# The last FFN's second product by seven block products in three passes

## The chip, the cores and the metric

The kernel runs on one core of one Trainium2 chip. Five engines of that core appear in the profile: TensorE for matrix products (PE, with its weight loads as PEld), VectorE (DVE), ScalarE (ACT), GpSimd (POOL) and SyncE (SP), whose queue issues nearly all the DMA transfers. The metric is the device time of one execution in microseconds (us).

## The reference

The program is a trunk of two layers on 512 tokens of width 1024: a gated short convolution, an FFN, a state-space mixer and a second FFN, each between two RMS norms and scaled, shifted and gated from a conditioning vector. All values are float32. The change touches the last FFN alone:

```python
def swiglu_ffn(h, w_in, w_out):
    gate, up = jnp.split(h @ w_in, 2, axis=-1)
    return (jax.nn.silu(gate) * up) @ w_out
...
        h = rmsnorm(x, norm_g[i, 2]) * (1.0 + scale) + shift
        y = swiglu_ffn(h, f_w_in[i], f_w_out[i])
        x = x + gate * rmsnorm(y, norm_g[i, 3])
```

The hidden width is 2816. The first product is 512 x 1024 by 1024 x 5632 (gate and up together); the second is 512 x 2816 by 2816 x 1024.

## The kernel before, in words

**Products.** Every float32 matrix is used as a pair of float32r parts: hi, a rounded copy that ACT makes (L202 for weights, L829 for activations), and lo, the value less hi, a DVE subtraction (L203, L830). One block product is then three matmuls: hi by hi, hi by lo and lo by hi. A matmul takes a 128 x 128 stationary block and a moving block of up to 512 columns and adds into one PSUM tile of 128 x 512.

**First product.** The 2816 hidden channels are 22 chunks of 128. `ffn` takes them in 11 pairs; a pair needs two gate chunks and two up chunks, and each chunk (`in_chunk`, L272, lines L259 to L261) is 8 x 3 matmuls of 512 tokens against the weight tile `whl`, channels on the partitions. `load_w` (L205) loads 256 columns of the weights as one 1 MB transfer into a `wst` tile (two buffers) and splits it into two `whl` tiles (four buffers). After a chunk, ACT takes the silu (L826), DVE multiplies gate by up (L827), and ACT and DVE split the product into the tiles `ff` (L829, L830), which all stay in SBUF. The first gate and up chunks of the stage are begun while the layer before still ends, and their matmuls have a line of their own (`li`).

**Second product.** `out_begin` (L346) goes over the two halves of 512 output columns. For each half and each of the 22 chunks, `mm_tiles` (L353, lines L359 to L361) multiplies four token tiles of 128 (stationary, from `ff`) with a weight block of 128 x 512 (moving, from `whlo`): 2 x 22 x 4 x 3 = 528 matmuls. `load_wo` (L226) loads `f_w_out` in pieces of up to four chunks into `wsto` tiles (the `wst` buffers) and splits them into `whlo` tiles (the `whl` buffers). The last two chunks of the first half and the last four of the second are done token tile by token tile (L502), and after each tile ACT squares and sums both halves (L400), DVE multiplies by gate and norm weight (L404), takes the reciprocal root (L414 on ACT, L417) and adds to the residual (L421), and SP stores the rows (L423).

**Order.** Within PE's part the order is as the code writes it; in the closing part of a stage it is written out by hand for PE, ACT and DVE. Elsewhere a scheduler orders each engine's queue and inserts the waits. An engine runs its queue in order, so an instruction that waits holds all that stand behind it; this goes for the transfers on SP's queue too.

## Time and profile before

| what | value |
|---|---|
| time, median of 3 runs | 1392.14 us (1391.38 to 1392.56) |
| span of the profiled execution | 1390.8 us |
| mean granted TensorE clock | 0.996 |
| PE busy | 1368.9 us of the span |
| DVE busy, ACT busy | 832.2 us, 552.4 us |
| DMA | 190.35 MB, mean 137 GB/s |
| matmuls of both FFNs' second products (L359 to L361, `y<-whlo,ff`) | 3 x 352 |

A row of a group of instructions gives line, engine, operation, written tile <- read tiles, shape and count; then the busy time in us, the mean duration of one in ns, and the idle time just before them with what ended it. Matmuls overlap: a matmul's duration in such a row is longer than the distance from one start to the next, so costs of PE are taken from starts. A row of the view by stretches of time gives the stretch, its length, the busy time and count of each engine, the granted clock (1.00 is full), the share of the 16 DMA engines and the GB/s. A row of the view of waits says who waited for whom: us in total, times, longest.

### The profile page before, as it was taken

The page shows a single profiled execution, that of the slowest core. Times are in us where ns is not written, and L with a number is a line of the kernel's source. Part 1 is how long each engine was busy: PE and PEld are TensorE (multiplying, and loading weights), DVE is VectorE, ACT ScalarE, POOL GpSimd, SP SyncE. Part 2 cuts the span into 40 slices and gives each one's busy share as a digit, 9 for nine tenths or more (in the row PEclk, how much of TensorE's full clock was granted, in tenths as well). Part 3 has the DMA queues.
Part 4 walks back from the last instruction along what each step waited for, and adds up shares of the span by engine and source line. Part 5 has one row for each costly group of instructions (what it writes and reads, how often), then busy time and mean ns, then how long its engine had stood idle before and what let it go on. Part 6 is the DMA issues. An engine that isn't in the chain of part 4 may idle for free.

```text
span 1390.8 us, 17396 instructions
## 1 busy us (share of the span) xinstructions
PE 1368.9 (98%) x7039; PEld 1148.8 (83%) x7039; DVE 832.2 (60%) x1332; ACT 552.4 (40%) x827; POOL 1.5 (0%) x11
## 2 busy tenths in 40 slices
PE   8999999999999999999799999999999999999998
PEld 7788889888888888898688888888898888888886
DVE  5777756488775222759878888876673333332224
ACT  5432247222222211745765466643573222322212
POOL 0000000000000000000000000000000000000000
PEclk9999999999999999999999999999999999999999
DMA  9956671368683223415244432423413223322221
GB/s 313 317 175 223 221 239 42 120 210 287 219 272 122 91 91 98 118 48 179 70 133 136 129 98 83 131 76 107 137 60 106 91 91 101 109 93 91 91 91 61
DMA packets 154037, 190.35 MB, mean 137 GB/s; under 512 B 5845, under 2 KB 110949, under 8 KB 152933
## 3 DMA queue, kind: packets, MB, share of 16 engines
q1 hardware_dynamic: 149952, 176.47, 39.2%
q10 hardware_dynamic: 4004, 12.77, 2.8%
q8 instruction: 55, 0.90, 0.3%
q14 instruction: 26, 0.20, 0.1%
HBM read 186.98 MB, written 2.24 MB: 136 GB/s over the span
## 4 chain that ended last, share of the span: by engine, by line
PE 66%; DVE 1%; issue 0%; DVEq 0%; ACT 0%; ACTq 0%
PE ip L259 11%; PE ip L261 11%; PE ip L260 11%; PE y L359 8%; PE y L360 8%; PE y L361 8%; PE li L259 2%; PE li L261 2%; PE li L260 2%; PE yd L1092 1%; PE yo L1086 1%; PE cb L1036 1%; PE xtr L460 1%; PE ssg L1114 0%; PE xtok L1019 0%; PE st L1051 0%
## 5 line engine op out<-in xcount | busy, mean ns | idle before, releaser
L259 PE MATMUL ip<-h,whl 128*128 128x512 f32 x1096 | 434.2, 396 | 2.7 <-DVE cv L777 2.7
L261 PE MATMUL ip<-h,whl 128*128 128x512 f32 x1096 | 429.4, 392 | 6.6 <-DVE whl L203 6.6
L260 PE MATMUL ip<-h,whl 128*128 128x512 f32 x1096 | 428.2, 391 | 0.0
L261 PEld LDWEIGHTS ip<-h,whl 128*128 128x128 f32 x1096 | 206.6, 188 | 50.7 <-DVE whl L203 7.0
L259 PEld LDWEIGHTS ip<-h,whl 128*128 128x128 f32 x1096 | 206.8, 189 | 47.7 <-issue 5.6
L260 PEld LDWEIGHTS ip<-h,whl 128*128 128x128 f32 x1096 | 206.7, 189 | 43.2 <-issue 1.2
L203 DVE TENSOR_TENSOR whl<-wst,whl 128x1024 fp32r<-128x1024 f32 (+1 forms) x163 | 177.2, 1103 | 101.4 <-ACT whl L202 101.2
L202 ACT CAST whl<-wst 128x1024 fp32r<-128x1024 f32 (+1 forms) x163 | 152.1, 951 | 201.0 <-PE ip L261 121.6
L203 DVE TENSOR_TENSOR whlo<-wsto,whlo 128x1024 fp32r<-128x1024 f32 x68 | 83.3, 1225 | 181.3 <-ACT whlo L202 181.3
L202 ACT CAST whlo<-wsto 128x1024 fp32r<-128x1024 f32 x68 | 71.5, 1051 | 200.6 <-PE y L361 162.2
L359 PE MATMUL y<-whlo,ff 128*128 128x512 f32 x352 | 137.0, 389 | 0.0
L361 PE MATMUL y<-whlo,ff 128*128 128x512 f32 x352 | 136.9, 389 | 0.0
L360 PE MATMUL y<-whlo,ff 128*128 128x512 f32 x352 | 136.9, 389 | 0.0
L126 DVE SCALAR_TENSOR_TENSOR ada_acc<-ada_st,csil,ada_acc 128x512 f32<-128x512 f32 x140 | 104.8, 750 | 22.9 <-DMA ada_st<-in_ada_w_dram 20.0
L259 PE MATMUL li<-h,whl 128*128 128x256 f32 x288 | 83.2, 289 | 0.0
L827 DVE TENSOR_TENSOR g<-ip,g 128x512 f32<-128x512 f32 x40 | 27.6, 691 | 92.5 <-PE ip L261 92.4
L261 PE MATMUL li<-h,whl 128*128 128x256 f32 x288 | 81.6, 283 | 0.0
L260 PE MATMUL li<-h,whl 128*128 128x256 f32 x288 | 81.5, 283 | 0.0
L826 ACT ACTIVATE g<-ip 128x512 f32<-128x512 f32 x36 | 21.6, 599 | 145.9 <-PE ip L261 145.9
L361 PEld LDWEIGHTS y<-whlo,ff 128*128 128x128 f32 x352 | 66.1, 188 | 13.8
L359 PEld LDWEIGHTS y<-whlo,ff 128*128 128x128 f32 x352 | 66.1, 188 | 13.7
L360 PEld LDWEIGHTS y<-whlo,ff 128*128 128x128 f32 x352 | 66.1, 188 | 13.6
(215 smaller groups left out, 1623.2 us busy)
## 6 DMA issues: line engine op xcount, KB each, us to landing
ada_st<-in_ada_w_dram SPq DMA_DIRECT2D x96, 512.0 KB, 5.8
wst<-in_f_w_in_dram SPq DMA_DIRECT2D x44, 1024.0 KB, 5.2
wsto<-in_f_w_out_dram SPq DMA_DIRECT2D x20, 1024.0 KB, 4.9
wst<-in_m_w_in_dram SPq DMA_DIRECT2D x14, 1024.0 KB, 5.4
wst<-in_m_w_in_dram SPq DMA_DIRECT2D x20, 512.0 KB, 5.0
wst<-in_a_w_in_dram SPq DMA_DIRECT2D x9, 1024.0 KB, 6.2
csb<-cs_d ACTq DMA_DIRECT2D x8, 1024.0 KB, 6.2
wsto<-in_m_w_out_dram SPq DMA_DIRECT2D x7, 1024.0 KB, 4.9
```

The costliest lines, as they stand in the source:

```text
L126: dve.scalar_tensor_tensor(acc, w, csil[:, k:k + 1], acc, MUL, ADD)
L202: act.copy(dst[:, 0, :nk, :], src)
L203: dve.tensor_tensor(dst[:, 1, :nk, :], src, dst[:, 0, :nk, :].bitcast(F32), SUB)
L259: pe.matmul(dst, w_at(w, 0, kk), a[:, 0, sl], start=start, stop=False)
L260: pe.matmul(dst, w_at(w, 0, kk), a[:, 1, sl], start=False, stop=False)
L261: pe.matmul(dst, w_at(w, 1, kk), a[:, 0, sl], start=False, stop=stop)
L359: pe.matmul(pst, a[:, 0, tk], wt[:, 0, kk, :], start=k == 0, stop=False)
L360: pe.matmul(pst, a[:, 0, tk], wt[:, 1, kk, :], start=False, stop=False)
L361: pe.matmul(pst, a[:, 1, tk], wt[:, 0, kk, :], start=False, stop=k == K - 1)
L460: pe.transpose(pt[:, j * 256 + t * P:j * 256 + (t + 1) * P], self.xn[2 * hi + t][p // 2][:, c:c + P], ident)
L826: act.activation(g, psg, AF.Silu)
L827: dve.tensor_mul(g, psu, g)
```

## The change

`ffn(3, ...)` is replaced by a function `last_ffn`. Its first product has the same matmuls. Its second product is seen as a product of 2 x 2 blocks: tokens 0 to 255 and 256 to 511, even and odd chunks of the hidden width, left and right half of the output columns. Strassen's algorithm in Winograd's form makes it from seven block products in place of eight, with sums of blocks of both factors ahead and sums of products behind. A block product over one pair of chunks is two token tiles of 128 by one weight block of 128 x 512, with three matmuls each.

- **Activations** (`ff_pair`, L1260): for each pair of chunks DVE multiplies gate by up straight into tiles `za` and `zb` (L1269 to L1271) and makes four sums of 128 x 256 (L1273 to L1276). They stay whole here; the split into hi and lo comes later, and the `ff` splits (L829, L830) are gone.
- **Weights**: for each pair of chunks SP loads the four blocks of `f_w_out` into a `tb` tile (L1284, L1285; two buffers), DVE makes four sums in place (L1291 to L1294), and SP stores the tile to device memory as `td` (L1297). This goes on beside the first product.
- **Second product**: 22 items of 18 matmuls (L1386 to L1388). Pass one, items 0 to 10, holds three of the seven products in the accumulators `pa`, `pb`, `pz`, pass two, items 11 to 21, three more; pass three adds the seventh product, 66 matmuls, onto `pb`, one token tile after the other. Per item SP loads `r8` (two blocks, 512 KB) and `r4` (one block, 256 KB) from `td` or `f_w_out`; ACT and DVE split the three left factors (`a6`, 128 x 768), `r8` into `w8` and `r4` into `w4` (L1321 on ACT, L1322 on DVE). Items are made four ahead (`AHEAD`). In pass one the left factors of pass three (`a22`, 128 x 256) are split as well, in pass two its weights (`t4`, three pairs of chunks per loading).
- **Between passes**: after pass one ACT copies `pa` (negated, `np1`) and `pz` (`c22`) and DVE takes `nr1` = `np1` - `pb`; after pass two DVE takes `nr2` from `pb` (L1429). The remaining sums (L1442, L1443, L1479) and the norm, gate, residual and stores stand beside and behind pass three.

PE runs 5975 instruction rows instead of 6041: 528 matmul rows of the second product become 22 x 18 + 66 = 462, and no other row of PE differs.

SP's queue in the first product (`wst` are its weight tiles, `tb` and `td` the new tiles; on each row, the written tile <- the read one). Before, weight loads stood one behind the other:

```order
L211 DMA wst<-in_f_w_in_dram 128x8x256 x4
L301 DMA gg<-gate_d 128x1024
L211 DMA wst<-in_f_w_in_dram 128x8x256 x15
L229 DMA wsto<-in_f_w_out_dram 128x4x512 x9
```

Now:

```order
L211 DMA wst<-in_f_w_in_dram 128x8x256 x4
L1284 DMA tb<-in_f_w_out_dram 128x2x512
L1285 DMA tb<-in_f_w_out_dram 128x2x512
L1284 DMA tb<-in_f_w_out_dram 128x2x512
L1285 DMA tb<-in_f_w_out_dram 128x2x512
L1297 DMA td_8572<-tb 128x2048
L1297 DMA td_8573<-tb 128x2048
L1284 DMA tb<-in_f_w_out_dram 128x2x512
L1285 DMA tb<-in_f_w_out_dram 128x2x512
L211 DMA wst<-in_f_w_in_dram 128x8x256
L1284 DMA tb<-in_f_w_out_dram 128x2x512
L1285 DMA tb<-in_f_w_out_dram 128x2x512
```

A load of `tb`, a store of `td` and a load of `wst` now alternate until the eleven tiles are stored; the last six loads of `wst` stand in one row again.

DVE's queue at the end of the first product. `za` and `zb` with `ip` or `g` behind the arrow are the last pair's products and sums; `w_10033` and `w_10032` are item 0's `w4` and `w8`, `w_10049` and `w_10048` those of item 1, `a_10047` item 1's `a6`. Before, from the last pair's product on:

```order
L827 TENSOR_TENSOR g<-ip,g 128x512
L203 TENSOR_TENSOR whlo<-wsto,whlo 128x1024
L830 TENSOR_TENSOR ff_9908<-g,ff_9908 128x512
L203 TENSOR_TENSOR whlo<-wsto,whlo 128x1024 x18
```

Now:

```order
L1322 TENSOR_TENSOR w_10033<-r_10028,w_10033 128x512
L1271 TENSOR_TENSOR zb<-ip,g 128x2x256
L1322 TENSOR_TENSOR w_10032<-r_10027,w_10032 128x1024
L1273 TENSOR_TENSOR za<-zb 128x256
L1322 TENSOR_TENSOR a_10040<-zb,a_10040 128x256
L1274 TENSOR_TENSOR za<-za 128x256
L1276 TENSOR_TENSOR zb<-za,zb 128x256
L1275 TENSOR_TENSOR zb<-za,zb 128x256
L1322 TENSOR_TENSOR a_10047<-za,a_10047 128x768
L1322 TENSOR_TENSOR w_10049<-r_10044,w_10049 128x512
L1322 TENSOR_TENSOR w_10048<-r_10043,w_10048 128x1024
```

The last pair's product with `ip` waits for the last matmul of the first product; the split of item 0's `w8` stands behind it, and the last pair's sums stand between it and item 1's splits.

DVE's queue at the end of pass two (`w_10748`, `w_10769`, `w_10793` are weights of pass three, loaded together as `t_10723`; `nr` are the two `nr2`):

```order
L1322 TENSOR_TENSOR w_10748<-t_10723,w_10748 128x512
L1322 TENSOR_TENSOR w_10769<-t_10723,w_10769 128x512
L1322 TENSOR_TENSOR w_10793<-t_10723,w_10793 128x512
L1429 TENSOR_TENSOR nr_10796<-np_10440,pb 128x512
L1429 TENSOR_TENSOR nr_10798<-np_10441,pb 128x512
L1322 TENSOR_TENSOR w_10802<-t_10790,w_10802 128x512
L1322 TENSOR_TENSOR w_10805<-t_10790,w_10805 128x512
```

Nothing of this stood there before. PE's first matmul of pass three writes `pb` and waits for `nr2`, which stands behind three splits that wait for the loading of `t_10723`.

The diff, cut:

```diff
--- before.py
+++ after.py
@@ -1246,10 +1246,243 @@
...
+    def last_ffn(begun, pool):
+        w1, w2 = f_w_in[1], f_w_out[1]
+        h, lead_ps, rest, more = begun
+        lo, hi = HALVES
+        NG2 = NF // 2
+        za, zb = [], []
+        td = [dram.tile([P, 4, T], F32, name=f"td{g}") for g in range(NG2)]
+        built = []
+        def ff_pair(pss):
+            a = pool.tile([P, 3, 256], F32, tag="za", name="za", bufs=NG2)
+            b = pool.tile([P, 4, 256], F32, tag="zb", name="zb", bufs=NG2)
+            gs = []
+            for i in range(2):
+                g = t2("g")
+                act.activation(g, pss[i], AF.Silu)
+                gs.append(g)
+            dve.tensor_mul(a[:, 0, :], pss[2][:, lo], gs[0][:, lo])
+            dve.tensor_mul(b[:, 1, :], pss[2][:, hi], gs[0][:, hi])
+            dve.tensor_mul(b[:, 0:4:3, :], pss[3].rearrange("p (a f) -> p a f", a=2),
+                           gs[1].rearrange("p (a f) -> p a f", a=2))
+            dve.tensor_tensor(a[:, 1, :], b[:, 1, :], b[:, 3, :], SUB)
+            dve.tensor_tensor(a[:, 2, :], a[:, 1, :], a[:, 0, :], SUB)
+            dve.tensor_tensor(b[:, 2, :], a[:, 2, :], b[:, 0, :], ADD)
+            dve.tensor_tensor(b[:, 1, :], a[:, 0, :], b[:, 1, :], SUB)
+            za.append(a)
+            zb.append(b)
+        def build_load(g):
+            st = pool.tile([P, 4, T], F32, tag="tb", name="tb", bufs=2)
+            w = w2[2 * g * P:(2 * g + 2) * P, :]
+            dma(st[:, 0:4:2, :], w[:, T:].rearrange("(a p) f -> p a f", p=P))
+            dma(st[:, 1:4:2, :], w[:, :T].rearrange("(a p) f -> p a f", p=P))
+            built.append(st)
+        def build_sums(g):
+            st = built[g]
+            b12, b11, b22, b21 = (st[:, i, :] for i in range(4))
+            dve.tensor_tensor(b11, b11, b12, ADD)
+            dve.tensor_tensor(b12, b12, b22, ADD)
+            dve.tensor_tensor(b22, b22, b11, ADD)
+            dve.tensor_tensor(b21, b21, b22, ADD)
+        def build_store(g):
+            dma(td[g], built[g])
+        for f in range(0, NF, 2):
+            g = f // 2
+            if f == 0:
+                with tc.manual_schedule(engines={PE_ENGINE}):
+                    for i in (0, 2, 1, 3, 4, 5):
+                        rest(i)
+                pss = lead_ps[:4]
+            elif f == 2:
+                pss = lead_ps[4:] + [in_chunk(w, h) for w in more]
+            else:
+                pss = [in_chunk(w, h) for w in load_w([(w1, f * P, 256)]) + load_w([(w1, DFF + f * P, 256)])]
+            build_load(g)
+            if g:
+                build_store(g - 1)
+            ff_pair(pss)
+            build_sums(g)
+        build_store(NG2 - 1)
+        def rows(g, b):
+            return slice((2 * g + b) * P, (2 * g + b + 1) * P)
+        def parts(src, dst):
+            act.copy(dst[:, 0], src)
+            dve.tensor_tensor(dst[:, 1], src, dst[:, 0].bitcast(F32), SUB)
+        ring = [0]
+        def wide(shape, dtype, name):
+            ring[0] += 1
+            if ring[0] % 2:
+                return wst_p.tile(shape, dtype, tag="wst", name=name)
+            return pool.tile(shape, dtype, tag="tb", name=name, bufs=2)
...
+        def load(i):
+            b, g = divmod(i, NG2)
+            r8 = hp.tile([P, 2, T], F32, tag=f"h{(2 * i + 1) % KD}", name="r8")
+            r4 = t2("r4")
+            if b == 0:
+                dma(r8, td[g][:, 1:3, :])
+                dma(r4, w2[rows(g, 0), :T])
+            else:
+                dma(r8, w2[rows(g, 1), :].rearrange("p (a f) -> p a f", a=2))
+                dma(r4, td[g][:, 0, :])
+            raws[i] = r8, r4
+        def make(i):
+            b, g = divmod(i, NG2)
+            r8, r4 = raws.pop(i)
+            a6 = wide([P, 2, 3, 256], F32R, "a6")
+            w8 = whl_p.tile([P, 2, 2, T], F32R, tag="whl", name="w8")
+            w4 = hp.tile([P, 2, T], F32R, tag=f"h{2 * i % KD}", name="w4")
+            parts((zb[g][:, 0:3, :] if b else za[g]), a6)
+            if b:
+                parts(r8, w8)
+                parts(r4, w4)
+            else:
+                parts(r4, w4)
+                parts(r8, w8)
+            if b == 0:
+                a22 = pool.tile([P, 2, 256], F32R, tag="za", name="a22", bufs=NG2)
+                parts(zb[g][:, 3, :], a22)
+                a22s.append(a22)
+            ready[i] = a6, w8, w4
+        def t4_load(g0):
+            st = wide([P, 3, T], F32, "t4")
+            for g in range(g0, min(g0 + 3, NG2)):
+                dma(st[:, g - g0, :], td[g][:, 3, :])
+                t4s.append(st[:, g - g0, :])
+        def t4_make(g):
+            w4 = pool.tile([P, 2, T], F32R, tag="zb", name="w4", bufs=NG2)
+            parts(t4s[g], w4)
+            w4s.append(w4)
+        def product(acc, a, w, first, ts=(0, 1)):
+            for t in ts:
+                sl = slice(t * P, (t + 1) * P)
+                pe.matmul(acc[t], a[:, 0, sl], w[0], start=first, stop=False, skip_group_check=True)
+                pe.matmul(acc[t], a[:, 0, sl], w[1], start=False, stop=False, skip_group_check=True)
+                pe.matmul(acc[t], a[:, 1, sl], w[0], start=False, stop=True, skip_group_check=True)
+        AHEAD = 4
+        with tc.manual_schedule(engines={PE_ENGINE, mybir.EngineType.Activation, mybir.EngineType.DVE}):
+            pa = [aux_ps("pa") for _ in range(2)]
+            pb = [aux_ps("pb") for _ in range(2)]
+            pz = [mm_ps("pz") for _ in range(2)]
+            for i in range(AHEAD):
+                load(i)
+                make(i)
+            for i in range(2 * NG2):
+                b, g = divmod(i, NG2)
+                a6, w8, w4 = ready.pop(i)
+                w8 = [(w8[:, 0, j, :], w8[:, 1, j, :]) for j in range(2)]
+                w4 = (w4[:, 0, :], w4[:, 1, :])
+                if b == 0:
+                    todo = [(pa, 0, w4), (pb, 2, w8[1]), (pz, 1, w8[0])]
+                else:
+                    todo = [(pa, 0, w8[0]), (pb, 1, w4), (pz, 2, w8[1])]
+                if i == 2 * NG2 - 1:
+                    todo = [todo[1], todo[0], todo[2]]
+                for acc, j, w in todo:
+                    product(acc, a6[:, :, j, :], w, i == 0)
+                if i == NG2 - 1:
+                    np1, nr1, c22 = ([keep(n) for _ in range(2)] for n in ("np1", "nr1", "c22"))
+                    for t in range(2):
+                        act.activation(np1[t], pa[t], AF.Copy, scale=-1.0)
+                    for t in range(2):
+                        dve.tensor_tensor(nr1[t], np1[t], pb[t], SUB)
+                    for t in range(2):
+                        act.copy(c22[t], pz[t])
+                if i + AHEAD < 2 * NG2:
+                    load(i + AHEAD)
+                    make(i + AHEAD)
+                if b and g >= 1 and g % 3 == 1 and len(t4s) < NG2:
+                    t4_load(g - 1)
+                if b and g >= 2 and g - 2 < len(t4s):
+                    t4_make(g - 2)
+            nr2s = []
+            for t in range(2):
+                nr2 = t2("nr2")
+                dve.tensor_tensor(nr2, np1[t], pb[t], SUB)
+                nr2s.append(nr2)
+            gg = wide([P, D], F32, "gg")
+            dma(gg, gate_d[3].rearrange("j p -> (j p)").partition_broadcast(P))
+            while len(t4s) < NG2:
+                t4_load(len(t4s))
+            while len(w4s) < NG2:
+                t4_make(len(w4s))
+            for t in range(2):
+                for g in range(NG2):
+                    product(pb, a22s[g], (w4s[g][:, 0, :], w4s[g][:, 1, :]), False, (t,))
+            for t in range(2):
+                dve.tensor_tensor(c22[t], nr2s[t], c22[t], ADD)
+                dve.tensor_tensor(nr1[t], nr1[t], pz[t], ADD)
+            ys = [(pa[0], nr1[0]), (pa[1], nr1[1]), (np1[0], c22[0]), (np1[1], c22[1])]
...
+            def root(t, hf):
+                s1 = small(1)
+                act.activation(s1, s2[t][:, hf:hf + 1], AF.Sqrt, bias=b1[t], scale=1.0 / D)
+                dve.reciprocal(s1, s1)
+                for hf in range(2):
+                    c = slice(hf * T, (hf + 1) * T)
+                    dve.scalar_tensor_tensor(xt[t][:, c], yg[t, hf], s1, xt[t][:, c], MUL, ADD)
+                    dma(out[0, t * P:(t + 1) * P, c], xt[t][:, c])
+            for t in range(2):
+                for hf in range(2):
+                    sq(t, hf)
+                    mul(t, hf)
+                bias(t, 0)
+                root(t, 1)
+            for t in (2, 3):
+                sq(t, 1)
+                mul(t, 1)
+                bias(t, 1)
+            for t in (2, 3):
+                dve.tensor_tensor(np1[t - 2], pb[t - 2], np1[t - 2], SUB)
+                sq(t, 0)
+                mul(t, 0)
+                root(t, 0)
     with ExitStack() as ph:
-        actp3 = ph.enter_context(tc.tile_pool(name="actp3", bufs=22, reuse_waits="tile"))
-        ffn(3, 1, begun, lambda n: actp3.tile([P, 2, T], F32R, tag="a", name=n),
-            lambda: actp3.tile([P, D], F32, tag="gg", name="gg", bufs=1), None, lambda f: None, (), None, None)
+        last_ffn(begun, ph.enter_context(tc.tile_pool(name="lf", bufs=1, reuse_waits="tile")))
 
 
 # ---- launch: one core; inputs and outputs as the reference has them ----
```

More of the change, by code (lines that the diff above doesn't have):

```diff
@@ L1247, in trunk_kernel, with keep, sq, mul @@
             begun = out_finish(parts)
+    def last_ffn(begun, pool):
[67 more added lines that the diff above has]
+            return pool.tile(shape, dtype, tag="tb", name=name, bufs=2)
+        def keep(name):
+            return pool.tile([P, T], F32, tag="keep", name=name, bufs=6)
+        raws, ready, a22s, w4s, t4s = {}, {}, [], [], []
+        def load(i):
[96 more added lines that the diff above has]
+            ys = [(pa[0], nr1[0]), (pa[1], nr1[1]), (np1[0], c22[0]), (np1[1], c22[1])]
+            s2 = [small(2) for _ in range(4)]
+            b1 = [small(1) for _ in range(4)]
+            yg = {}
+            def sq(t, hf):
+                act.activation(t2("junk"), ys[t][hf], AF.Square, accum_out=s2[t][:, hf:hf + 1])
+            def mul(t, hf):
+                yg[t, hf] = t2("yg") if t < 2 or hf == 0 else ys[t][hf]
+                dve.tensor_mul(yg[t, hf], ys[t][hf], gg[:, hf * T:(hf + 1) * T])
+            def bias(t, hf):
+                dve.tensor_scalar(b1[t], s2[t][:, hf:hf + 1], 1.0 / D, EPS, MUL, ADD)
+            def root(t, hf):
[21 more added lines that the diff above has]
+                root(t, 0)
```

## The prediction

> **What bounds the kernel now.** I read the page's busy shares and chain first, then the view by stretches for the last FFN's two products, then the instructions in order of time at both ends of the second.
>
> ```profile
> span 1390.8 us, 17396 instructions
> PE 1368.9 (98%) x7039; PEld 1148.8 (83%) x7039; DVE 832.2 (60%) x1332; ACT 552.4 (40%) x827; POOL 1.5 (0%) x11
> PE 66%; DVE 1%; issue 0%; DVEq 0%; ACT 0%; ACTq 0%
> ...
> core 0: us, PE busy (x) PEld busy (x) DVE busy (x) ACT busy (x) POOL busy (x), PEclk, DMA share, GB/s
> 1056.00:1264.00 208.00, 208.00 (x925) 172.47 (x924) 71.23 (x77) 59.24 (x78) 0.00 (x0) 1.00 0.27 91
> 1264.20:1383.90 119.70, 119.70 (x529) 98.91 (x527) 33.94 (x41) 27.42 (x38) 0.00 (x0) 1.00 0.24 81
> ```
>
> The chain is PE's. In the last FFN PE is never idle: first product (first row of the stretches, to 1264) and second product (second row) are full at clock 1.00, while DVE is busy 34% and 28% of them, ACT 28% and 23%, DMA 27% and 24%. So here PE's matmuls can be sold for DVE, ACT and DMA work, as long as that work is on time.
>
> ```profile
> 1264.23 0.39 PE L359 MATMUL y<-whlo,ff 128*128 128x512 f32 x1
> ...
> 1383.68 0.39 PE L361 MATMUL y<-whlo,ff 128*128 128x512 f32 x1
> ```
>
> These are the first and the last of the second product's 528 matmuls: 119.45 us over 527 steps, 0.2267 us each (0.39 is the modelled length of one, which overlaps the next).
>
> **What is removed.** 528 matmuls become 22 items of 18 and 66 more, 462. Stationary and moving blocks keep their shapes and the three matmuls of a block their order, so I take the same step: 66 x 0.2267 = 15.0 us less, all on the path. An item lasts 18 x 0.2267 = 4.08 us, a pair of chunks of the first product (96 matmuls) 21.8 us.
>
> **What is added, by duration.**
>
> ```profile
> L203 DVE TENSOR_TENSOR whlo<-wsto,whlo 128x1024 fp32r<-128x1024 f32 x22 | 27.0, 1226 | 84.3 <-ACT whlo L202 84.3
> L830 DVE TENSOR_TENSOR ff<-g,ff 128x512 fp32r<-128x512 f32 x22 | 15.0, 685 | 2.5 <-ACT ff L829 2.5
> L478 DVE TENSOR_TENSOR h<-u,h 128x256 fp32r<-128x256 f32 x48 | 19.5, 422 | 18.4 <-ACT h L474 18.1
> L202 ACT CAST whlo<-wsto 128x1024 fp32r<-128x1024 f32 x22 | 23.2, 1053 | 86.2 <-PE y L361 74.5 <-issue 7.8 <-PE ip L261 3.9
> L829 ACT CAST ff<-g 128x512 fp32r<-128x512 f32 x22 | 13.5, 616 | 0.0
> L474 ACT CAST h<-u 128x256 fp32r<-128x256 f32 x48 | 18.5, 404 | 10.8 <-DVE u L469 10.1
> ```
>
> No row has 768 columns; between 512 and 1024 I take the middle, 0.96 on DVE and 0.83 on ACT.
>
> *First product.* Per pair DVE makes three products (0.42 + 0.42 + 0.69), four sums of 256 (1.7), four of 512 (2.7) and the four `whl` splits of before (4 x 1.23 = 4.9): 10.9 of 21.8 us. PE covers it. On SP's queue the loads of `wst` now stand behind `tb` and `td`. One weight tile takes load, sums, store:
>
> ```profile
> wst<-in_f_w_in_dram SPq DMA_DIRECT2D x44, 1024.0 KB, 5.2
> wsto<-in_f_w_out_dram SPq DMA_DIRECT2D x20, 1024.0 KB, 4.9
> wst<-in_m_w_in_dram SPq DMA_DIRECT2D x20, 512.0 KB, 5.0
> wst_l<-in_a_w_in_dram SPq DMA_DIRECT2D x9, 256.0 KB, 8.1
> ecsb<-ecs_d ACTq DMA_DIRECT2D x16, 256.0 KB, 5.9
> wsto<-in_f_w_out_dram SPq DMA_DIRECT2D x4, 512.0 KB, 3.7
> out_dram<-x SPq DMA_DIRECT2D x8, 256.0 KB, 2.0
> ...
> SPq L211 <- DVE whl L203: 165.4, 15, 19.4
> ```
>
> 4.9 + 2.7 + 4.9 (a store of this size isn't in the trace; I take the load's) = 12.5 us, and two run at once, so 6.3 us per tile against 21.8 per pair. The last row says that SP waited 11 us on average, 19.4 at most, for a `wst` buffer: loads are held by buffers, not by SP. A load that must follow a store and another tile's sums starts some 10 us later than it could; its weights are used more than one pair (21.8 us) after the buffer comes free. Cost nothing; without that cover a late load costs its landing and two splits, 5.2 + 1.05 + 1.23 = 7.5 us.
>
> *Passes.* DVE needs for an item of pass one 0.96 + 1.23 + 0.69 + 0.42 = 3.3 us, of pass two (with a `t4` split) 3.6; ACT 2.9 and 3.1. Both are under 4.08. An item's buffers come free when the item four before ends; the splits then take ACT 0.83 and DVE behind it, about 4.6 us in all, and PE asks for them 3 x 4.08 = 12.2 us later. That leaves 7.6 us. Loading is 768 KB per item, in pass two up to 1 MB with `t4`: 193 to 257 GB/s. The trace has done more:
>
> ```profile
> 30.00:40.00 10.00, 9.87 (x101) 7.68 (x100) 4.49 (x12) 3.84 (x6) 0.00 (x0) 1.00 1.09 351
> ```
>
> Cost nothing. Between the passes `np1` and `nr1` read `pa` and `pb` 2.7 us before the item ends, which is enough for 2 x 0.62 on ACT and 2 x 0.69 on DVE.
>
> *Start of the second product.* Here the cover is gone. Let 0 be when PE could issue the first matmul of item 0; another engine sees a matmul 0.55 us after its step ends (L361 above starts at 1383.68, ACT behind it at 1384.46, next fence). `r8` of item 0 goes into the place of `h1`, free after 6 of the last chunk's 24 matmuls, at -4.08 + 0.55 = -3.5. Its 512 KB land 3.7 us later (the row of `f_w_out`, 512 KB), at 0.2; ACT's part is ready at 1.3. DVE must first take the last pair's product (0.55 to 1.24), then splits `w8`: ready at 2.6. PE meanwhile does `pa` (6 matmuls, 1.36 us) and one more, and stands from 1.6 to 2.7: 1.1 us. DVE goes on with five operations of 256 (2.1), item 1's `a6` (0.96) and `w4` (0.69), until 6.4; PE wants that `w4` at 5.4: 1.0 us more. Item 2's come at 10.1, item 3's at 13, when PE is at 10.3 and 14.4, and DVE gains 0.8 us per item from there. Sum 2.1 us. From both sides: landing sooner changes little, since DVE's product at 1.24 then decides (1.8); landing in 5.0 (`m_w_in`, 512 KB) adds 1.3 (3.4); in 6.2, another 1.2.
>
> *Start of pass three.* `pb` waits for `nr2`, which on DVE stands behind three `t4` splits. That loading starts when item 19 ends. Two further items, 8.16 us, pass on PE. Landing at 3.7 to 4.4 us, ACT 0.62 and DVE 3 x 0.69 behind it bring DVE to 6.3, `nr2` to 7.0. Nothing; with 5.9 us for 256 KB (the `ecsb` row) 1.2 us.
>
> *Tail.*
>
> ```profile
> 1384.46 0.60 ACT L400 ACTIVATE junk<-y 128x512 f32<-128x512 f32 x1 [2.38 <-PE y L361]
> 1384.95 0.19 ACT L400 ACTIVATION_READ_ACCUMULATOR junk<-y 128x1 f32 x1
> 1385.18 0.69 DVE L404 TENSOR_TENSOR yg<-y,gg 128x512 f32<-128x512 f32 x1 [1.50 <-ACT junk L400]
> 1385.79 0.15 DVE L417 RECIPROCAL ss<-ss 128x1 f32<-128x1 f32 x1
> 1385.98 1.41 DVE L421 SCALAR_TENSOR_TENSOR x<-yg,ss,x 128x512 f32<-128x512 f32 x2
> ```
>
> Before, the square and then the multiplication by `gg` follow the last matmul, 2.93 us to the end of L421. Now the sum L1479 (0.69) comes first, but square and multiplication then read SBUF and run side by side, so I count 0.5 us, between 0 and 0.7. The other token tiles end 7.5 us or more before.
>
> **Sum.** -15.0 + 2.1 + 0 + 0.5 = -12.4 us: the profiled execution would go from 1390.8 to 1378.4. The median of the runs stands 1.3 above that span, so 1379.8.
>
> **Rivals.**
>
> *The start stalls longer and the clock drops.*
>
> ```profile
> PE ip L261 <- DVE whl L203: 6.6, 1, 6.6
> PE ip L259 <- DVE cv L777: 2.7, 1, 2.7
> ...
> PE cb L1036 <- DVE xdt L1025: 0.7, 1, 0.7
> ...
> 64.00:65.00 1.00, 0.34 (x2) 1.00 1.09 387
> 65.00:66.00 1.00, 1.00 (x4) 0.52 1.07 375
> ...
> 68.00:69.00 1.00, 1.00 (x5) 0.77 1.11 352
> 69.00:70.00 1.00, 1.00 (x7) 1.00 1.03 375
> ```
>
> The view of PE's waits and single microseconds behind the second of them (stretch, PE busy, granted clock, DMA share, GB/s): after 2.7 us without work PE ran at half clock from about 65 to 68.5, which is 1.7 us lost; the wait of 0.7 shows no such loss. My two gaps of 1.1 and 1.0 lie near the harmless one. If `r8` lands 2.5 us later, the first gap is 3.6, the clock drops, and the start costs 3.6 + 1.0 + 1.7 = 6.3: 1384.0. For it: four transfers of 512 KB leave within 4 us. Against it: 3.7 us is what this very matrix needed.
>
> [...]
>
> *Preparation paces the passes (slower).* If DVE did not overlap ACT, because each split waits for the cast just ahead of it, an item would last 6.2 us in pass one and 6.7 in pass two: 11 x 2.1 + 11 x 2.6 = 52 us more, 1432. It decides against the change from 4.08 + 12.4 / 22 = 4.65 us per item. For it: DVE is at 80 to 87% of PE's pace. Against it: ACT runs ahead in its own queue by whole items, and DVE's 1024 columns took the same 1.22 where the DMA engines were busy, early in the program:
>
> ```profile
> L203 DVE TENSOR_TENSOR whlo<-wsto,whlo x8: 1215/1224/1226, 152.7 to 191.1; 128x1024 fp32r<-128x1024 f32 x8
> ```
>
> *SP starves the first product (slower).* If for two of the pairs the loads waited until their chunk is due, 2 x 7.5 = 15 us: 1395; from 12.4 us on the gain is gone. For it: one queue in order, two waits per tile. Against it: 6.3 against 21.8 us.
>
> PE's queue has the 66 rows less, so that the work isn't removed is no rival.
>
> **How the numbers follow.** Forecast 0.73, clock drop or a late `r8` 0.14, pacing 0.06, starving 0.05, some other loss that leaves it near before 0.02. About 0.2% (2.8 us) is what a measurement here can tell from no change; the first two cases lie beyond it, and a mild form of pacing or starving too: faster 0.89, same 0.04, slower 0.07. Range: the forecast's own best is start 1.8 and tail 0, 1379; less 0.7, about what the lowest of the three runs lies below their median, 1378.3. Above it reaches past the clock drop with pass three's 1.2 and the tail's 0.7 on it, 1386.
>
> **What would show it.** Right: matmuls of L1386 to L1388 at 0.2267 us; two waits of about 1 us on L1322 splits at the start of item 0's `pb` and item 1's `pa`, granted clock 1.00 behind them; no wait of PE in the first product nor from item 3 on; last matmul to end of span about 7.4 us. Wrong: waits of PE on L203 (starving), on L1322 in every item (pacing), on L1429 (pass three), or a clock of 0.5 behind the start.

## The result, and the profile after

The median went from 1392.35 us (1391.38 to 1394.56, 4 runs) to 1380.16 us (1377.61 to 1380.77, 4 runs): ratio 0.9908, 95% interval 0.9894 to 0.9922, so 12.2 us or 0.9% faster. The profiled execution went from a span of 1390.8 to 1377.5 us.

The page of the changed kernel, its head and the start of its chain; then, with the columns of the prediction's table of stretches, the first product, the second from its first matmul to the end of its last, and the second's three passes by themselves:

```profile
span 1377.5 us, 17633 instructions
PE 1353.7 (98%) x6973; PEld 1135.5 (82%) x6973; DVE 911.7 (66%) x1485; ACT 580.6 (42%) x875; POOL 1.5 (0%) x11
...
PE 64%; DVE 2%; DMA 1%; ACT 0%; issue 0%; SPq 0%; DVEq 0%; ACTq 0%
...
1056.00:1264.00 208.00, 208.00 (x925) 172.49 (x924) 97.22 (x145) 46.79 (x55) 0.00 (x0) 1.00 0.55 188
1264.00:1370.15 106.15, 105.31 (x463) 86.32 (x461) 84.34 (x119) 68.20 (x108) 0.00 (x0) 1.00 0.56 191
1264.00:1309.00 45.00, 44.16 (x194) 35.87 (x193) 40.36 (x55) 34.92 (x52) 0.00 (x0) 1.00 0.78 263
1309.00:1355.20 46.20, 46.20 (x206) 38.26 (x205) 31.75 (x40) 27.14 (x41) 0.00 (x0) 1.00 0.46 159
1355.20:1370.15 14.95, 14.95 (x67) 12.19 (x65) 12.24 (x26) 6.14 (x16) 0.00 (x0) 1.00 0.19 72
```

The chain is still PE's. The first product is still full on PE, with DVE up from 34% to 47% busy and DMA from 91 to 188 GB/s. The second product is 106 us long instead of 119.7, with DVE at 79% and ACT at 64%. In pass one DVE is at 90%, yet PE is idle for only 0.84 us there; passes two and three are full. The granted clock is 1.00 throughout. PE's matmul records in the trace went from 7039 to 6973, the 66 fewer that the change has.

Where PE stood, in order of time (start, duration, then in brackets the idle time and what ended it; the last row is the end of the second product):

```profile
1263.93 0.39 PE L1386 MATMUL pa<-w,a 128*128 128x512 f32 x1
...
1265.29 0.40 PE L1386 MATMUL pb<-w,a 128*128 128x512 f32 x1
1266.41 0.50 PE L1387 MATMUL pb<-w,a 128*128 128x512 f32 x1 [0.72 <-DVE w L1322]
...
1269.05 0.39 PE L1386 MATMUL pa<-w,a 128*128 128x512 f32 x1
1269.56 0.50 PE L1387 MATMUL pa<-w,a 128*128 128x512 f32 x1
...
1369.92 0.39 PE L1388 MATMUL pb<-w,a 128*128 128x512 f32 x1
```

A step is 0.2267 us, so the first stop is 1266.41 - 1265.29 - 0.23 = 0.89 us and the second 1269.56 - 1269.05 - 0.23 = 0.28. From first to last matmul are 105.99 us; 461 steps at 0.2267 make 104.49; so 1.50 us are lost, the two stops and 0.3 in the steps right behind them. There is no other wait of PE in the last FFN.

### The profile page after: what moved, and what is told of

The parts are those of the page before. It is cut to its first block, busy times and chain, and to the rows that moved or that the text cites. A ratio compares the mean times of both kernels' runs of the same rounds, so it can differ in the third digit from the quotient of the medians.

```text
span 1377.5 us, 17633 instructions
## 1 busy us (share of the span) xinstructions
PE 1353.7 (98%) x6973; PEld 1135.5 (82%) x6973; DVE 911.7 (66%) x1485; ACT 580.6 (42%) x875; POOL 1.5 (0%) x11
## 4 chain that ended last, share of the span: by engine, by line
PE 64%; DVE 2%; DMA 1%; ACT 0%; issue 0%; SPq 0%; DVEq 0%; ACTq 0%
PE ip L259 11%; PE ip L261 11%; PE ip L260 11%; PE y L359 5%; PE y L361 5%; PE y L360 5%; PE li L259 2%; PE li L261 2%; PE li L260 2%; PE yd L1092 1%; PE yo L1086 1%; PE pa L1387 1%; PE pa L1388 1%; PE pz L1388 1%; PE pb L1388 1%; PE pz L1386 1%
## 5 line engine op out<-in xcount | busy, mean ns | idle before, releaser
L203 DVE TENSOR_TENSOR whlo<-wsto,whlo 128x1024 fp32r<-128x1024 f32 x46 | 56.3, 1223 | 96.6 <-ACT whlo L202 96.6
L202 ACT CAST whlo<-wsto 128x1024 fp32r<-128x1024 f32 x46 | 48.3, 1050 | 113.6 <-PE y L361 87.7
L957 DVE SCALAR_TENSOR_TENSOR cu<-ip,cols,cu 128x511 f32<-128x511 f32 (+2 forms) x84 | 62.0, 741 | 13.7 <-ACT cu L954 13.5
L359 PE MATMUL y<-whlo,ff 128*128 128x512 f32 x176 | 68.6, 390 | 0.0
L361 PE MATMUL y<-whlo,ff 128*128 128x512 f32 x176 | 68.5, 389 | 0.0
L360 PE MATMUL y<-whlo,ff 128*128 128x512 f32 x176 | 68.5, 389 | 0.0
L259 PEld LDWEIGHTS li<-h,whl 128*128 128x128 f32 x288 | 55.3, 192 | 0.0
L260 PEld LDWEIGHTS li<-h,whl 128*128 128x128 f32 x288 | 55.2, 192 | 0.0
L261 PEld LDWEIGHTS li<-h,whl 128*128 128x128 f32 x288 | 55.1, 191 | 0.0
L359 PE MATMUL y<-whlo,ys 128*128 128x512 f32 x128 | 51.1, 399 | 0.0
```

Source lines behind the costliest of these rows:

```text
L202: act.copy(dst[:, 0, :nk, :], src)
L203: dve.tensor_tensor(dst[:, 1, :nk, :], src, dst[:, 0, :nk, :].bitcast(F32), SUB)
L259: pe.matmul(dst, w_at(w, 0, kk), a[:, 0, sl], start=start, stop=False)
L260: pe.matmul(dst, w_at(w, 0, kk), a[:, 1, sl], start=False, stop=False)
L261: pe.matmul(dst, w_at(w, 1, kk), a[:, 0, sl], start=False, stop=stop)
L359: pe.matmul(pst, a[:, 0, tk], wt[:, 0, kk, :], start=k == 0, stop=False)
```

## The experiments

In each, "lost" is the time from the first to the last matmul of the second product less the steps between them at 0.2267 us, taken from that run's trace. It does not contain what varies elsewhere in the program between single executions (1377.6 to 1380.8 for the changed kernel). r8h3, r8h5, r8h7, ring1 and dve2 were executed once each.

### What the matmuls alone are worth

```diff
 (b66: the kernel before, mm_tiles)
+                    if s != 3 or hf or t == 3:
-                    pe.matmul(pst, a[:, 0, tk], wt[:, 1, kk, :], start=False, stop=False)
+                        pe.matmul(pst, a[:, 0, tk], wt[:, 1, kk, :], start=False, stop=False)
```

> The kernel before, with 66 of the second product's 528 matmuls left out: in the first half of the columns, token tiles 0 to 2 go without the product of the activations' high part with the weights' low part (3 tiles x 22 chunks), so the output lacks these terms. No other engine's work changes. Theory (what is removed): 66 x 0.2267 = 15.0 us less than before, so about 1377.4 us, ratio 0.989; the changed kernel (1380.2) then stands 2.8 us above it, and that is the price of everything that was added: the two gaps at the start (0.89 + 0.28 + what else is lost there, together about 1.5) and the tail (0.5), and what lies between single executions. Rival (part of the gain has another source, for example a first product that now runs faster): the removal alone is worth less, 1379 us or more.

Measured: 1378.04 us, ratio 0.9895 (0.9881 to 0.9910), against 1393.05 for the kernel before: 15.0 us less. In the trace:

```profile
1263.77 0.39 PE L359 MATMUL y<-whlo,ff 128*128 128x512 f32 x1
...
1368.26 0.39 PE L362 MATMUL y<-whlo,ff 128*128 128x512 f32 x1
```

That is 104.49 us for 461 steps; nothing lost. Removal is worth its full count, and the gain needs no other source. The changed kernel stands some 2 us above this one.

The mirror of it (p66), the changed kernel with as many matmuls as before:

```diff
-            for t in range(2):
+            for t in (0, 1, 0, 1):
                 for g in range(NG2):
                     product(pb, a22s[g], ...
```

> The changed kernel with pass three done twice, so 66 matmuls more; the seventh product is counted twice in the output. All preparation (loads, sums, splits) stays as it is. Theory (the gain is the removed matmuls and nothing else): 15.0 us more than the changed kernel, about 1395.2 us, which is 2.8 us slower than before: with the number of matmuls equal, only what was added is left. Rival (the passes are paced by DVE and ACT and the removed matmuls were not what set the time): the second round of pass three needs no preparation, so it would still cost its 15 us, but the passes ahead of it would show waits of PE on the splits L1322 in most items; the theory expects such waits only in items 0 and 1.

Measured: 1394.00 us, ratio 1.0008 (0.9999 to 1.0017). From first to last matmul 120.95 us against 119.45 before: lost 1.50, the same two stops at the start and nothing else. The mechanism is the expected one. The 1.0 us by which it stands above before is less than the 2.8 forecast, and the interval of its ratio does not exclude that there is no difference; one part of the miss is known, the tail, which cost nothing in this version (below).

### The start of the second product

In the changed kernel, item 0's `r8` landed when PE had begun the second product. ACT's cast of it waits for the transfer, DVE's split for the cast, and item 1's `w4` (the first operation of the last row) stands behind both in DVE's queue:

```profile
1264.04 1.05 ACT L1321 CAST w<-r 128x1024 fp32r<-128x1024 f32 x1 [4.05 <-DMA r<-td]
...
1265.13 1.22 DVE L1322 TENSOR_TENSOR w<-r,w 128x1024 fp32r<-128x1024 f32 x1 [0.31 <-ACT w L1321]
...
1268.82 1.82 DVE L1322 TENSOR_TENSOR w<-r,w 128x512 fp32r<-128x512 f32 x2
```

Three runs make this `r8` later by giving it another place, one more takes the place away from the question:

```diff
 (r8h3; r8h5 and r8h7 with 5 and 7)
-            r8 = hp.tile([P, 2, T], F32, tag=f"h{(2 * i + 1) % KD}", name="r8")
+            r8 = hp.tile([P, 2, T], F32, tag=f"h{(2 * i + 3) % KD}", name="r8")
 (early)
+            if i < 2:
+                r8 = pool.tile([P, 2, T], F32, tag="keep", name="r8", bufs=3)
+            else:
+                r8 = hp.tile([P, 2, T], F32, tag=f"h{(2 * i + 1) % KD}", name="r8")
```

> The changed kernel, but r8 of every item takes the place of h3, h5, ... instead of h1, h3, ...; for item 0 that place is freed 6 matmuls (1.36 us) later in the last chunk of the first product, so its load leaves 1.36 us later. Theory (item 0's r8 sets the first gap): the first wait of PE on L1322, 0.89 us in the changed kernel, becomes about 2.2; the second (0.28) shrinks or stays; span 1.0 to 1.4 us longer, 1378.5 to 1378.9; the granted clock stays 1.00, as the gap is under the 2.7 us behind which the kernel before shows half clock. Rival (DVE's queue sets the gap, not the landing): the first wait stays at 0.9.

> As the run before, with h5 for item 0's r8: its load leaves 2.72 us later than in the changed kernel. Theory: first wait of PE about 3.6 us. That lies above the 2.7 us behind which the kernel before showed half clock, so a granted clock of 0.5 for about 3.5 us behind it, 1.7 us lost: span about 1377.5 + 2.7 + 1.7 - 0.3 = 1381.6. This is the rival of the clock drop, brought about on purpose. [...]

> As the run before, with h7 for item 0's r8: its load leaves 4.08 us later than in the changed kernel. Theory: first wait of PE about 5.0 us, a granted clock of 0.5 for about 3.5 us behind it, span 1377.5 + 4.1 + 1.7 - 0.3 = 1383.0. Rival (no clock drop): 1381.3.

> The changed kernel, but r8 of items 0 and 1 gets tiles of its own (those that np1, nr1 and c22 use later) instead of the places of h1 and h3, so that it is loaded and split while PE is still in the first product. Theory (the start's cost is the late r8 of items 0 and 1 and DVE's queue behind it): both gaps of PE (0.89 and 0.28, and up to 0.3 more that the step lost there) vanish, 1.2 to 1.5 us less than the changed kernel: a span near 1376.1, median about 1378.8, ratio to the kernel before 0.990. Rival (something else is late at the same place, for example DVE's last product of the first product or the loads of item 1): PE waits there on another tile and the time stays within 0.5 us of the changed kernel.

| run | first stop | second stop | half clock | lost | span |
|---|---|---|---|---|---|
| changed kernel | 0.89 | 0.28 | none | 1.50 | 1377.5 |
| r8h3 | 1.66 | 1.03 | 3.4 us | 4.44 | 1380.8 |
| r8h5 | 4.78 | 0.81 | 6.8 us | 8.27 | 1384.8 |
| r8h7 | 5.55 | 0.81 | 6.8 us | 8.81 | 1385.5 |
| early | none | none | none | 0.00 | 1374.8 |

A stop is counted here as what exceeds a step at the clock of the moment. In the changed kernel the two stops are item 0's split of `w8` and item 1's `w4`; in the three late runs they are ACT's cast of item 0's `r8` and DVE's split behind it, and by item 1 nothing is late any more. The late `r8` is shown to be the cause: later, the first stop grows; early, both vanish, 1263.09 to 1367.58 is 104.49 us without a wait, and the median is 1378.57 us, ratio 0.9896 (0.9879 to 0.9913).

Two expectations missed, and the three spans lie 1.9 to 3.2 us above what was expected. First, the stops do not grow by 1.36 us a step. The edit also turned the order in which SP issues these loads (a load whose place is free earlier goes first), so item 0's 512 KB stand behind one, two or three others; ACT's cast of it starts 0.1 us after PE's first matmul in the changed kernel, and 1.9, 5.0 and 5.8 us after it in the three runs. Second, r8h3 was to keep its clock, since neither stop comes near 2.7 us. It did not. Its stretches of 3.41 us, the length of the half clock behind the wait of 2.7 us in the kernel before, 65.05 to 68.46 us there (stretch, PE busy with matmul count, granted clock, DMA share, GB/s):

```profile
1259.90:1263.32 3.42, 3.42 (x16) 1.00 0.52 177
1263.32:1266.73 3.41, 2.91 (x13) 1.00 0.95 296
1266.73:1270.14 3.41, 1.66 (x6) 1.00 0.79 274
1270.14:1273.56 3.42, 3.42 (x10) 0.50 0.97 341
1273.56:1276.97 3.41, 3.41 (x16) 1.00 0.76 243
```

The clock falls at 1270.14, when PE has long been at work again, and stays at half for one stretch of 3.41 us, in which half the work is done: 1.71 us lost. 1.66 + 1.03 + 1.71 is the 4.44, but for 0.04. In the stretch ahead of the fall, 1266.73 to 1270.14, lie the second stop and 1.0 us of the first, which had begun at 1266.07: 1.66 us of PE work are left in it. In r8h5 and r8h7 the first stretch at half clock had only 5 and 3 matmuls (2.30 and 1.80 us), and the clock stayed at 0.50 for a second one.

### The passes: how much cover there is, and what it is worth

```diff
 (ring2: a6 in two buffers, two items ahead)
-            ring[0] += 1
-            if ring[0] % 2:
+            if name == "a6":
                 return wst_p.tile(shape, dtype, tag="wst", name=name)
-        AHEAD = 4
+        AHEAD = 2
 (ring1: a6 in one buffer, one item ahead, one build tile in the first product)
+            if name == "a6":
+                return pool.tile(shape, dtype, tag="a6", name=name, bufs=1)
+            return wst_p.tile(shape, dtype, tag="wst", name=name)
-        AHEAD = 4
+        AHEAD = 1
-            st = pool.tile([P, 4, T], F32, tag="tb", name="tb", bufs=2)
+            st = pool.tile([P, 4, T], F32, tag="tb", name="tb", bufs=1)
 (dve2: DVE's splits of w4 and w8 done twice)
+            again(r4, w4)
+            again(r8, w8)
```

> The changed kernel with two buffers for the split activation parts a6 instead of four, and preparation two items ahead instead of four (the other two wide buffers are left to t4 and gg). The cover of the step on the passes shrinks from three items (12.2 us) to one (4.08 us). Theory (the chain behind a freed buffer is about 0.55 + 0.83 on ACT + 0.96 + 0.69 on DVE = 3.0 us in pass one, and 0.55 + 0.83 + 0.96 + 1.23 = 3.6 in pass two, both under 4.08): no wait of PE in the passes beyond the start's, and the time of the changed kernel within 1 us, 1379.2 to 1381.2. Rival (preparation paces the passes; DVE and ACT do not overlap, 6.2 to 6.7 us an item): waits of about 2 us in every item, 1425 us or more.

> The changed kernel with a single buffer for a6, preparation one item ahead, t4 and gg in the wst buffers, and one buffer instead of two for the first product's build tile. Now no item covers the chain behind a freed buffer. Theory: PE waits about 3.0 us ahead of each item of pass one and 3.6 us ahead of each of pass two, on splits of L1322: 10 x 3.0 + 11 x 3.6 = 70 us more, a span near 1447; if the granted clock halves behind gaps of this length as it did behind the 2.7 us gap of the kernel before (1.7 us lost each time), up to 21 x 1.7 = 36 us on top, 1483. Rival (ACT and DVE have slack enough that even this hides, because ACT starts on the next item while PE still reads the old one): under 1400. In the first product one build tile takes 12.5 us (4.9 + 2.7 + 4.9) of 21.8 us per pair, so no wait of PE there by theory; starving would show a wait of PE on L203.

> The changed kernel with DVE's splits of w4 and w8 done twice for every item (the second time with the same result), 0.60 + 1.14 = 1.74 us more DVE work per item. DVE's rows of the changed kernel start 2.94 us apart per item in pass one and need 2.7 in pass two, 3.4 with a t4 split; with the addition 4.68, 4.4 and 5.1, against PE's 4.08. Theory (preparation paces the passes as soon as DVE's item is longer than PE's): PE waits in nearly every item, (4.68 - 4.08) x 11 + (4.4 - 4.08) x 11 + 0.68 x 6 = 14 us in all, less what the items prepared ahead cover; a span of 1387 to 1393, so that about nothing is left of the gain, as the prediction's limit of 4.65 us per item says. The granted clock stays at 1.00, since PE still works 80% or more of each few microseconds. Rival (ACT and DVE do not overlap, as the slower case of the prediction had it, and only the lead hides it now): far more, 1400 or above. Rival (DVE's time is hidden anyway): within 1 us of the changed kernel.

**ring2**: 1379.18 us, ratio 0.9902 (0.9885 to 0.9918), lost 1.56. One item of cover in place of three costs nothing, as expected. In the changed kernel, DVE's splits of two items of pass one that follow each other are 2.94 us apart, against PE's 4.08:

```profile
1268.82 1.82 DVE L1322 TENSOR_TENSOR w<-r,w 128x512 fp32r<-128x512 f32 x2
...
1271.76 1.81 DVE L1322 TENSOR_TENSOR w<-r,w 128x512 fp32r<-128x512 f32 x2
```

**ring1**: 1468.45 us, span 1466.7, lost 90.8. Inside the range, and its two parts can be separated. The waits of PE in it:

```profile
PE pa L1385 <- ACT w L1321: 33.5, 20, 2.4
PE pa L1386 <- DVE w L1322: 13.3, 20, 0.8
```

In pass one an item takes 6.67 us (from one such wait's end to the next), 2.6 more than 4.08; 3.0 was forecast. The first product, with a single build tile, shows no wait of PE, which answers the starving rival. The rest is the clock. Here every stretch of 3.41 us, laid end to end from 1263.16 on, has a single clock, 1.00 or 0.50; some of them:

```profile
1266.57:1269.99 3.42, 2.66 (x12) 1.00 0.96 362
1269.99:1273.40 3.41, 1.39 (x6) 1.00 0.53 202
1273.40:1276.81 3.41, 3.41 (x10) 0.50 0.74 186
1276.81:1280.23 3.42, 1.98 (x9) 1.00 0.11 44
...
1290.47:1293.88 3.41, 1.87 (x8) 1.00 0.36 123
1293.88:1297.29 3.41, 2.93 (x13) 1.00 0.37 107
1297.29:1300.71 3.42, 1.72 (x7) 1.00 0.32 123
1300.71:1304.12 3.41, 3.09 (x7) 0.50 0.45 154
```

A stretch at full clock with 8 matmuls or more (a full one shows 16 or 17, as those across its edges count too) was followed by one at 1.00 here, one with 7 or fewer by one at 0.50, in all 34 at full clock up to 1444 (other runs have exceptions, see the end). 19 stretches ran at half clock with 59 us of PE work in them, so about 30 us of the 91 are the clock's.

**dve2**: 1403.70 us, span 1401.9, lost 23.2; a span of 1387 to 1393 was expected. From item 3 of pass one on, the items are 4.68 us apart, exactly DVE's steps, so there the theory was right in kind. The time lies where the first rival had put it (1400 or above), but by the slower case that it names an item would take more than 6.2 us. What the expectation had left out is the first and the last of these rows, and the clock:

```profile
1267.84 0.50 PE L1392 MATMUL pa<-w,a 128*128 128x512 f32 x1 [3.02 <-DVE w L1325]
...
1292.24 0.50 PE L1392 MATMUL pa<-w,a 128*128 128x512 f32 x1 [0.29 <-DVE w L1325]
1296.92 0.50 PE L1392 MATMUL pa<-w,a 128*128 128x512 f32 x1 [0.30 <-DVE w L1325]
...
1331.10 0.79 PE L1391 MATMUL pb<-w,a 128*128 128x512 f32 x1 [8.08 <-DVE nr L1421]
```

The start stops PE for 3.0 us; between the passes PE waits 8.1 us for `nr1`, which stands in DVE's queue behind the splits of the next items; and behind both the granted clock fell (means of 0.67 over 1268 to 1272 and of 0.50 over 1328 to 1332). The 7.6 us that were expected in pass two did not come: behind the wait of 8.1 us its items take 4.08 us again, up to the last. The tail is 9.5 us, 2.2 longer than in the changed kernel. By the prediction's limit of 4.65 us per item the gain would be just spent at 4.68; measured, it is overspent by 10 us, since a late DVE meets the boundary between the passes too. In the changed kernel that boundary has this much room:

```profile
1309.99 1.28 DVE L1416 TENSOR_TENSOR nr<-np,pb 128x512 f32<-128x512 f32 x2
...
1311.66 0.39 PE L1386 MATMUL pb<-w,a 128*128 128x512 f32 x1
...
1312.34 0.39 PE L1386 MATMUL pb<-w,a 128*128 128x512 f32 x1
```

`pb` is two tiles, one for each of the two `nr1` in the first row (0.68 us each, started 0.60 apart). The first tile is read out at 1310.67 and overwritten at 1311.66, the second at 1311.27 and 1312.34: 1.0 us. Ahead of pass three it is 0.9 us (`nr2`, below). The items' own splits end 4.5 us or more ahead of PE from item 5 on, so behind the start the two boundaries are the narrowest places of the passes.

### The tail, and a version without both losses

The tail of the changed kernel, DVE and ACT behind the last matmul, whose step ends at 1370.15:

```profile
1359.84 1.28 ACT L1461 ACT_TABLE_LOAD   x1 [1.72 <-DVE ss L1457]
...
1361.46 0.16 DVE L1462 RECIPROCAL ss<-ss 128x1 f32<-128x1 f32 x1 [1.70 <-ACT ss L1461]
...
1369.68 0.75 DVE L1465 SCALAR_TENSOR_TENSOR x<-yg,ss,x 128x512 f32<-128x512 f32 x1
1370.35 0.75 DVE L1465 SCALAR_TENSOR_TENSOR x<-c,ss,x 128x512 f32<-128x512 f32 x1
1371.01 0.68 DVE L1479 TENSOR_TENSOR np<-pb,np 128x512 f32<-128x512 f32 x1
```

L1479 of the last token tile could have started 0.2 us behind the step's end, and starts at 0.86: DVE is still finishing token tile 2. Until 1361.5 it had been idle for 1.70 us while ACT loaded its table for the square root; from there on it pauses only twice, 0.42 and 0.45 us, each time for a square root of ACT.

```diff
 (early2: early, and)
             while len(w4s) < NG2:
                 t4_make(len(w4s))
+            act.activation(small(1), eps_t, AF.Sqrt)
```

> The changed kernel with both of its measured losses attacked: r8 of items 0 and 1 in tiles of their own, as in the run before this, and one dummy square root on ACT ahead of the sums of pass three, so that the 1.28 us ACT_TABLE_LOAD, which in the changed kernel stands at 1359.84 between DVE's L1457 and L1462 with DVE idle for 1.70 us, happens while ACT is idle. Theory (the tail is longer because DVE is still at token tile 2's L1465 when the last matmul ends, and that backlog comes from the table load): L1479 of the last token tile starts 0.2 us after the last matmul's step ends instead of 0.86 us in the changed kernel; second product 104.5 us without a gap, tail 0.67 us shorter; together 2.1 us less than the changed kernel, a median near 1378. Rival (DVE's backlog has other causes and the last tile's chain is late anyway): only the start's 1.5 us are gained, and L1479 stays at 0.6 or more behind the last matmul.

> The changed kernel once more, beside the version that removes its two losses, against the same runs of the kernel before. Theory: ratio 0.991 as first measured, 2.1 us above the other version; in its trace the two gaps at the start (1.5 us in all) and the last L1479 at 0.86 us behind the last matmul. Rival (what the trace of a single execution showed at the start and the tail was that execution's own): the gaps or the late L1479 are not there.

Measured beside each other: 1377.93 us for the version without the losses, ratio 0.9895 (0.9880 to 0.9909); 1379.19 us for the changed kernel, ratio 0.9901 (0.9885 to 0.9918). That is 1.3 us apart, where 2.1 was forecast. The intervals overlap, so the times alone don't part the two; the traces do. Of the first:

```profile
1264.60 0.39 PE L1390 MATMUL pa<-w,a 128*128 128x512 f32 x1
...
1369.10 0.39 PE L1392 MATMUL pb<-w,a 128*128 128x512 f32 x1
...
1369.52 0.69 DVE L1484 TENSOR_TENSOR np<-pb,np 128x512 f32<-128x512 f32 x1 [0.48 <-PE pb L1392]
```

104.50 us, nothing lost, and the last tile's sum 0.19 us behind the step's end; the changed kernel's second profile lost 1.52 and had that sum 0.70 late. From the traces, relative to the end of the last matmul's step:

| kernel | table load before it | sum starts after it | to the end of the span (tail) |
|---|---|---|---|
| changed kernel | 10.30 | 0.86 | 7.33 |
| the same, second profile | 10.47 | 0.70 | 7.15 |
| early | 10.61 | 0.55 | 7.01 |
| p66 | 25.43 | 0.20 | 6.67 |
| ring2 | 11.33 | 0.19 | 6.66 |
| early2 | 15.78 | 0.19 | 6.66 |
| before (no such sum) | 11.33 | | 6.93 |

Tail less start is 6.5 in every row of the changed forms, so what differs between them is DVE's backlog alone. In the first three rows the backlog shrinks by as much as the table load stands earlier. It was absent where pass three lasted longer (p66) or the wide buffers were shared out differently (ring2, with the load 1 us earlier), and the square root's table ahead of time removes it (early2, which differs from early in nothing else). At 1377.93 us this version is as fast as the plain removal of 66 matmuls (1378.04; the ratio is 0.9895 for both): as far as these runs can tell, all that the change added is then hidden.

## Why the prediction was right, step by step

- **What is removed** (15.0): right. 104.49 us for 461 steps in the run with 66 matmuls left out, 15.0 us in its time.
- **First product** (0): right, with much room. The transfers took longer than assumed (the rows of `tb`, 512 KB, land in 6.9 us and not 3.7 to 4.9, `wst` in 6.7 and not 5.2; the store took the assumed 4.9), and still no wait of PE, not even with one build tile. DVE needed 97.2 us in the 208 of it, 10.2 a pair with 10.9 forecast.
- **Passes** (0): right, though by the wrong measure. The sums of durations, 3.3 and 3.6 us per item, overstate DVE: consecutive operations start closer than they last (a 256-column one every 0.34 us, lasting 0.42), and the items stand 2.94 apart in pass one. The cover of 7.6 us was real: with one item of cover there was still no wait, with none it cost 2.6 us an item of pass one and the clock. Between the passes the prediction had `pb` done 2.7 us before the item ends; that holds for `pa`, and for `pb` it is 1.4. The room there, for which "enough" was all the prediction said, was 1.0 us.
- **Start of the second product** (+2.1, measured +1.5): mechanism right, mis-sized. The first gap was 0.89 for 1.1 and the second 0.28 for 1.0. The term that was off is DVE's queue from item 0's split to item 1's `w4`, counted by durations: forecast ready at 6.4 us, in the trace 1269.51, which is 5.58. `r8` itself landed as thought, 0.1 us after PE's first matmul where 0.2 was forecast. The restarts, 0.3 in all, were not in the sum.
- **Start of pass three** (0): right; `nr2` ended 0.9 us ahead of PE, where 1.2 was worked out.
- **Tail** (+0.5, measured +0.4): the size was right by luck and the reason wrong. The sum, square and multiplication behind each other cost 0.14 us where DVE is free (3.62 us from the step's end to DVE's last operation, 3.48 before). DVE's backlog adds 0.66, and the end of the program is 0.40 shorter for a reason left open (below). What failed is "the other token tiles end 7.5 us or more before", which was true of PE alone: DVE finished tile 2 0.95 us after the last matmul.
- **The sum**: -15.0 + 1.5 + 0.4 makes -13.1 of the profiled executions' -13.4; the rest is the second product's start, 1263.93 for 1264.23, which moves by more than that between traces of the same work (1265.35 in p66, whose code is the changed kernel's up to pass three). That the median came within 0.4 us of the forecast is partly luck: single executions of the changed kernel lie 3.2 us apart.

**The rivals.** *The clock drops*: r8h3 is this rival, brought about. A cast 1.8 us later gave 1380.8, 3.3 above the changed kernel's span. The rival had put 2.5 us later at 4.2 above the forecast, and named a single gap of 3.6 us as the condition; two stops of 1.66 and 1.03 sufficed. The case was nearer than thought: in r8h3 half clock followed a stretch of 3.41 us with 6 matmuls, 1.66 us of PE work. In the changed kernel the stretch with the first stop (1265.60 to 1269.01) still has 12, 2.69 us of work. *Preparation paces the passes*: excluded here by ring2, and priced by dve2. *SP starves the first product*: excluded by ring1's single build tile.

## What to carry to other kernels

Work that leaves the engine on the critical path is worth its full step count only if the seams are fed too: all of this change's cost that could be traced lay in 1.5 us at the start and 0.4 at the end, where another engine's in-order queue was late, and both could be removed by moving the first two loads of `r8` and one table load earlier. To see how near an edit is to trouble, look for the least room at the seams (1.0 and 0.9 us at the two boundaries between the passes) and not at the mean busy share, and try an experiment that makes the suspected transfer later as well as one that makes it earlier. When a queue of one engine is costed, use the distance between starts, not the durations.

## What the runs showed of the hardware

- In the traces named here the granted clock was 1.00 or 0.50 over whole stretches of 3.41 us. In ring1 the 55 stretches laid end to end from 1263.16 to 1450.89 us have a single clock each. In the kernel before, half clock stands from 65.05 to 68.46 and from 689.69 to 696.51 us, in the changed kernel from 64.11 to 67.52 and from 688.74 to 695.57: one stretch and two in each. Their edges do not coincide with a stop's: the wait on `cv` ended 0.39 us ahead of the edge at 65.05 in the one, at 64.66, and 0.29 us behind the edge at 64.11 in the other, at 64.40. In ring1, a stretch at full clock with 8 or more matmuls of 512 columns (1.70 us of PE work or more) was followed by full clock, one with 7 or fewer (1.72 or less) by half. Elsewhere the count is not sharp: in the kernel before, the stretch from 1382.60 has 7 (PE busy 1.47 us), and the one behind it still had 1.00; in dve2, the 4 us from 1320 have 6 (1.94 us), and the 4 us behind them, without a matmul, still had a mean of 0.92. In ring1, a stretch at half clock with 2.88 us of PE work or more was followed by full clock, one with 2.81 or less by half.
- The same stop was followed by half clock in one trace, which is 1.7 us lost, and by full clock in another. The wait on `cv` at 64 us, which is no part of the change, was 2.55 us in the changed kernel and 2.53 in "early"; the stretch from 60 to 70 us, of the changed kernel and then of "early":

```profile
60.00:70.00 10.00, 7.45 (x29) 5.85 (x28) 10.00 (x15) 3.51 (x5) 0.00 (x0) 0.83 0.91 305
```

```profile
60.00:70.00 10.00, 7.47 (x35) 6.03 (x34) 10.00 (x15) 3.42 (x5) 0.00 (x0) 1.00 0.93 305
```

29 matmuls at a mean clock of 0.83 in one, 35 at 1.00 in the other. This is part of the scatter between single executions, and of the low span of "early".
- In the changed kernel, DVE operations in a row overlap by 0.08 us (256 columns: 0.42 us long, 0.34 apart; 512: 0.68 and 0.60), and the matmul behind the first stop takes 0.33 us to the next start (1266.41 to 1266.74) instead of 0.23.
- The end of the program, from DVE's last operation to the end of the span, is 3.45 us in the kernel before and 3.05 in the changed one (3.41 in dve2, a changed form too). No run tells why; it is left open.
